# One PSUM row for the last group's weighted sums, and a pair tile for each pair sum, at the end of a summed-area-table diagonal kernel

## The chip, the cores and the metric

The kernel runs on one core of one Trainium2 chip. The metric is the device time of one execution in microseconds (us); the median of several executions is quoted. The span of a profile is shorter than that time, mostly by about 1.7 us, so spans are compared with spans and times with times.

## The reference

```python
B, H, W = 4, 4224, 4224          # x: float32, normally distributed
ps = np.cumsum(np.cumsum(x, axis=1), axis=2)
diag = np.diagonal(ps, axis1=1, axis2=2)
return np.cumsum(diag, axis=1).astype(np.float32)      # 4 x 4224
```

Element (i, j) of a matrix enters every diagonal place k with k >= max(i, j), and so enters place n of the output n + 1 - max(i, j) times. The work is to read 285 MB once and add it up by max(i, j).

## The kernel before: the parts that matter

A strip of 768 rows is loaded as bf16 (the load converts: the page of before counts 285.47 MB read from memory and 143.27 MB in the packets, about half). TensorE sums its columns right of the diagonal block, ScalarE and VectorE sum its rows left of it, and a masked product by VectorE splits the diagonal block. The outputs are worked out in 11 groups of 384 places.

The last group of the last matrix has a path of its own, since nothing can follow its loads but what still has to be done with them. Its first 256 rows are `part_a` (two loads). Its last 128 rows are `part_b`: four blocks of 32 rows (0 to 3), each row spread over four partitions as 1024 columns. Blocks 0 to 2 have one load each, block 3 has two (768 columns, then 256). A row's total is multiplied by a row of weights in a matmul with one output partition ("weighing"), the products gather in PSUM (where this kernel's matmuls put their results, `fin_a`, `fin_m` and `fin_e` below), and VectorE adds the gathered row to what the earlier rows gave (`c12`) and hands it to the store.

```python
def act_sum(acc, src):                        # ScalarE: sum along a row
    ...
def pair_sum(acc, src):                       # VectorE: sum along a row, two halves at a time
    w = src.shape[-1] // 2
    pair = dumpool.tile([P, 512], FP32, name="pair")     # ONE buffer for all pair sums
    nc.vector.scalar_tensor_tensor(out=pair[:, :w], in0=src[:, :w], scalar=1.0,
        in1=src[:, w:], op0=ALU.mult, op1=ALU.add, accum_out=acc)

# ... rows before the last 128: folded by TensorE 128 columns at a time
fold_a = psum_s.tile([P, 2, P], FP32, name="fold_a")
fold_in(fold_a, part_a, c0, cp, P, start=True)
# ... cut: the two scans and the output of the earlier groups ...

fin_a = psum_s.tile([1, M0], FP32, name="fin_a")         # places 0..255
fin_m = psum_s.tile([1, E0 - M0], FP32, name="fin_m")    # places 256..351
fin_e = psum_s.tile([1, R], FP32, name="fin_e")          # places 352..383
# ... cut: block 0 and half of block 1 folded by TensorE with weights, result `by` ...
fins = ((fin_a, 0, M0), (fin_m, M0, E0), (fin_e, E0, GW))
weigh(arows[:, 0:1], weights, 0, fins[:1], start=True)
# ... six more calls, each of one matmul per row that it touches ...
finish(fin_a, 0, M0)                                     # VectorE: 256-place addition
act_sum(bsum[:, 1:2], part_b[:, 2, :448])                # block 2
pair_sum(bsum[:, 2:3], part_b[:, 2, 448:])
for k in (1, 2):
    weigh(bsum[:, k : k + 1], weights4, M0 + 2 * R, fins)

act_sum(esum[:, 0:1], part_b[:, 3, :320])                # block 3
pair_sum(esum[:, 1:2], part_b[:, 3, 320:bcut])           # "first pair sum"
pair_sum(esum[:, 2:3], part_b[:, 3, bcut:])              # "second pair sum", the last load
for k in (1, 0, 2):
    weigh(esum[:, k : k + 1], weights4, E0, fins)
finish(fin_m, M0, E0)
# ... store of places 0..351 ...
finish(fin_e, E0, GW)
# ... store of places 352..383, the last instruction but for the end
```

## Time and profile before

| | before |
|---|---|
| time, median of 6 runs | 668.55 us (668.1 to 669.11); 668.58 of the first three |
| span of the profiled run | 666.7 us |
| DMA engines | full in every slice of the page but the last (9, then 8 tenths), 428 GB/s read |
| last load's landing, to the issue of the last store | 663.753 to 664.765: 1.012 us |
| issue of the last store, to the end of the kernel | 1.943 us |

The third row says that nothing but the load matters until the last load lands. The two rows under it are all that a change at the end can shorten. A landing is read from the record of the semaphore that the load raises. The measure "landing of the last load to the issue of the last store" leaves out when the stream happened to end.

### The profile page before, as it was taken

Reading aid. Unit: us, or ns where it says so; the run is one execution under the profiler, and the core shown is the slowest. Engines: PE = TensorE matmul, PEld = TensorE weight load, DVE = VectorE, ACT = ScalarE, POOL = GpSimd, SP = SyncE. Lnnn points to the kernel's source line nnn. Section 1 sums busy time; section 2 is a strip of 40 time slices with the busy share of each in tenths; the row PEclk is TensorE's granted clock in tenths of the full one; section 3 lists DMA queues with packets and bytes.
Section 4 is the critical chain, followed back from the end, with each engine's and each line's share of the span. In section 5 each row is a group of like instructions: output and inputs, shape, how many; then the busy total and the mean of one; then the engine's idle time right before and its main releaser. Section 6 shows DMA issues by size and latency. Waiting matters only on the chain.

```text
span 666.7 us, 2921 instructions
## 1 busy us (share of the span) xinstructions
PE 215.4 (32%) x1009; PEld 99.4 (15%) x1009; DVE 335.7 (50%) x381; ACT 140.2 (21%) x226; POOL 28.0 (4%) x61
## 2 busy tenths in 40 slices
PE   0071623403118153140321724404032254350426
PEld 0030211101003021010110312201011021120103
DVE  3023627276924351745782425265498241635776
ACT  0000121406300103040630020304063002030436
POOL 5000000000000000000000000000000000001000
PEclk9995858566558585765655958667565595765759
DMA  9999999999999999999999999999999999999998
GB/s 201 219 219 219 214 219 218 211 217 213 218 220 219 216 217 219 216 217 219 214 216 216 216 219 217 220 211 219 217 217 219 213 220 215 217 217 217 215 210 154
DMA packets 7673, 143.27 MB, mean 215 GB/s; under 512 B 702, under 2 KB 1002, under 8 KB 2154
## 3 DMA queue, kind: packets, MB, share of 16 engines
q0 software_dynamic: 7296, 142.47, 99.8%
q1 hardware_dynamic: 362, 0.61, 0.3%
q8 instruction: 8, 0.13, 0.1%
q14 instruction: 7, 0.06, 0.0%
HBM read 285.47 MB, written 0.07 MB: 428 GB/s over the span
## 4 chain that ended last, share of the span: by engine, by line
another core or an unknown queue 39%; DVE 24%; PE 21%; DMA 12%; issue 4%; POOL 0%; DVEq 0%; POOLq 0%
PE d L214 21%; DVE acc L240 16%; DMA strip<-in_x_dram 12%; DVE mu L257 6%; POOL strip L420 0%; DVE pu L240 0%; DVE c L257 0%; POOL strip L409 0%; DVE acc L343 0%; DVE acc L340 0%; PE carry_ps L214 0%; DVE rows L368 0%; DVEq L257 0%; PE fin_e L214 0%
## 5 line engine op out<-in xcount | busy, mean ns | idle before, releaser
L257 DVE SCALAR_TENSOR_TENSOR mu<-strip,um 128x768 bf16<-128x768 bf16 (+1 forms) x129 | 110.7, 908 | 308.9 <-DMA strip<-in_x_dram 217.6
L214 PE MATMUL d<-strip,sel 128*11 128x384 bf16 x603 | 138.9, 404 | 333.8 <-DMA strip<-in_x_dram 333.8
L235 ACT ACTIVATE dump<-strip 128x416 bf16<-128x416 bf16 (+8 forms) x112 | 128.3, 1146 | 523.0 <-DMA strip<-in_x_dram 520.3
L240 DVE TENSOR_REDUCE acc<-strip 128x6 f32<-128x4608 bf16 (+6 forms) x23 | 195.9, 8519 | 0.0
L214 PEld LDWEIGHTS <-sel 128*11 128x11 bf16 x849 | 86.2, 102 | 512.9 <-issue 475.3
L214 PE MATMUL d<-mu,sel 128*11 128x384 bf16 x243 | 59.6, 354 | 65.7 <-DVE mu L257 65.5
L76 POOL DMA_DIRECT2D strip<-in_x_dram x24 | 16.4, 686 | 555.9 <-DVE acc L240 415.4
L235 ACT ACTIVATION_READ_ACCUMULATOR dump<-strip 128x1 f32 x112 | 20.9, 186 | 0.0
L214 PE MATMUL d<-ident,rows 128*11 128x128 f32 x24 | 5.2, 379 | 17.2 <-DVE rows L377 16.4
L257 DVE DVE_READ_ACCUMULATOR mu<-strip,um 128x1 f32 x129 | 10.6, 82 | 0.0
L214 PE MATMUL fold<-strip,ident_h 128*128 128x480 bf16 x8 | 3.3, 589 | 8.6 <-DMA strip<-in_x_dram 8.6
L214 PEld LDWEIGHTS d<-ident,rows 128*11 128x11 f32 x24 | 2.5, 119 | 19.1 <-DVE rows L377 17.3
L214 PE MATMUL d<-halves,rows 128*11 128x64 f32 x48 | 5.3, 290 | 0.0
L214 PEld LDWEIGHTS d<-halves,rows 128*11 128x11 f32 x48 | 4.7, 127 | 1.8 <-issue 1.7
L240 DVE TENSOR_REDUCE pu<-d 11x1 f32<-11x384 f32 x4 | 2.2, 545 | 5.0 <-PE d L214 5.0
L214 PE MATMUL fold<-weights,quarter 32*128 32x128 f32 x2 | 0.8, 498 | 11.0 <-POOL quarter L200 11.0
L447 DVE TENSOR_TENSOR_SCAN c<-ones_row,carry,c 11x384 f32<-11x384 f32 x4 | 4.0, 1006 | 0.1
L447 DVE TENSOR_TENSOR_SCAN c<-ones_row,carry,d 11x384 f32<-11x384 f32 x4 | 4.0, 1001 | 0.1
L214 PEld LDWEIGHTS <-ident_h 128*128 128x128 bf16 x20 | 2.2, 114 | 12.0 <-issue 11.9
L420 POOL DMA_DIRECT2D strip<-in_x_dram x5 | 2.7, 552 | 21.5 <-DMA strip<-in_x_dram 21.5
L240 DVE TENSOR_REDUCE parts<-strip 128x3 f32<-128x3072 bf16 x1 | 3.4, 3350 | 0.0
L221 DVE COPY weights<-fold 128x128 f32<-128x128 f32 x1 | 0.3, 291 | 5.4 <-PE fold L214 5.4
(102 smaller groups left out, 44.4 us busy)
## 6 DMA issues: line engine op xcount, KB each, us to landing
strip<-in_x_dram POOLq DMA_DIRECT2D x19, 6336.0 KB, 69.2
strip<-in_x_dram POOLq DMA_DIRECT2D x5, 3168.0 KB, 55.2
strip<-in_x_dram POOLq DMA_DIRECT2D x1, 1080.0 KB, 45.0
strip<-in_x_dram POOLq DMA_DIRECT2D x1, 768.0 KB, 48.0
strip<-in_x_dram POOLq DMA_DIRECT2D x3, 256.0 KB, 49.2
head<-in_x_dram SPq DMA_DIRECT2D x1, 528.0 KB, 3.9
strip<-in_x_dram POOLq DMA_DIRECT2D x1, 192.0 KB, 43.7
strip<-in_x_dram POOLq DMA_DIRECT2D x1, 64.0 KB, 28.6
```

The costliest lines, as they stand in the source:

```text
L76: nc.gpsimd.dma_start(out=o, in_=x[b, r0 : r0 + f * P, :].rearrange("(p f) w -> p f w", f=f))
L214: nc.tensor.matmul(o, lhsT=lhsT, rhs=rhs, start=start, stop=False, skip_group_check=True)
L221: nc.vector.tensor_copy(out=weights4, in_=w4_ps)
L235: nc.scalar.activation(out=dump[:, :w], in_=src, func=ACT.Copy, accum_out=acc)
L240: nc.vector.reduce_sum(out=acc, in_=src, axis=AX.X)
L257: nc.vector.scalar_tensor_tensor(out=o, in0=i, scalar=1.0, in1=m, op0=ALU.mult, op1=ALU.mult, accum_out=acc,)
L420: nc.gpsimd.dma_start(out=part_b[:, sb, c0:c1], in_=x[b, r0 : r0 + R, :TB].rearrange("r (k c) -> r k c", k=4)[:, :, c0:c1],)
L447: nc.vector.tensor_tensor_scan(out=c12[:, i, :], data0=ones_row, data1=src, initial=carry[:, i : i + 1], op0=ALU.mult, op1=ALU.add,)
```

## The change

The intent is to have less in front of the last pair sums. All weighted sums but block 3's gather in one PSUM row, so that each total is weighed by one matmul instead of up to three. The rows of `part_a` are folded 256 columns at a time (folding: TensorE adds slices of so many columns onto one another in PSUM, which leaves one slice for VectorE to sum up). Block 1 is summed by ScalarE and VectorE instead of half by TensorE. The addition of the first 256 places moves behind block 2's pair sum. Each pair sum writes a tile of its own.

```diff
+    pairs = []
     def pair_sum(acc, src):
         w = src.shape[-1] // 2
-        pair = dumpool.tile([P, 512], FP32, name="pair")
+        pair = last.tile([P, 288], FP32, name=f"pair{len(pairs)}")
+        pairs.append(pair)
@@ part_a
-            fold_a = psum_s.tile([P, 2, P], FP32, name="fold_a")
+            fold_a = psum_s.tile([P, 2, 256], FP32, name="fold_a")
-            fold_in(fold_a, part_a, c0, cp, P, start=True)
+            fold_in(fold_a, part_a, c0, cp, 256, start=True)
   (and the same for the second load)
@@ last group
-        fin_a = psum_s.tile([1, M0], FP32, name="fin_a")
-        fin_m = psum_s.tile([1, E0 - M0], FP32, name="fin_m")
+        fin = psum_s.tile([1, GW], FP32, name="fin")
   (weigh: one matmul into fin[:, r0:]; finish(c0, c1) adds fin[:, c0:c1])
-        c1a = CB // 2
-        for sb, cp in ((0, CB), (1, c1a)):
-            ... four matmuls of block 1 among them ...
+        for c in range(0, CB, P):
+            matmul(by_ps, part_b[:, 0, c : c + P], weights4_h, start=c == 0)
   ...
-        finish(fin_a, 0, M0)
-        act_sum(bsum[:, 1:2], part_b[:, 2, :448])
-        pair_sum(bsum[:, 2:3], part_b[:, 2, 448:])
-        for k in (1, 2):
-            weigh(bsum[:, k : k + 1], weights4, M0 + 2 * R, fins)
+        for k, ca in ((0, 512), (1, 448)):
+            act_sum(bsum[:, k, 0:1], part_b[:, k + 1, :ca])
+            pair_sum(bsum[:, k, 1:2], part_b[:, k + 1, ca:])
+            if k == 1:
+                finish(0, M0)
+            row_sums(btot[:, k : k + 1], bsum[:, k])
+            weigh(btot[:, k : k + 1], weights4, M0 + (k + 1) * R)
   ...
-            weigh(esum[:, k : k + 1], weights4, E0, fins)
-        finish(fin_m, M0, E0)
+            matmul(fin_e, esum[:, k : k + 1], weights4[:, :R], start=k == 1)
+        finish(M0, GW)
   ...
-        finish(fin_e, E0, GW)
+        ye = last.tile([1, R], FP32, name="ye")
+        nc.vector.tensor_add(out=ye, in0=fin_e, in1=yl[:, E0:])
```

## The prediction

> **What bounds the kernel now.** I read the page first: slices, queues, memory traffic.
>
> ```profile
> DMA  9999999999999999999999999999999999999998
> q0 software_dynamic: 7296, 142.47, 99.8%
> q8 instruction: 8, 0.13, 0.1%
> HBM read 285.47 MB, written 0.07 MB: 428 GB/s over the span
> ```
>
> The reader is to see that the DMA engines are full in every slice: the load of x is 285.47 MB, and 285.47 MB at 428 GB/s is the whole span of 666.7 us. VectorE is busy 50%, TensorE 32%. So the change, which touches only the last group of the last matrix, cannot move the body. All that is left to it is the stretch between the landing of the last loads and the end. The table by windows shows how short that is (its columns are span, then busy time and count of TensorE, weight loads, VectorE, ScalarE, GpSimd, then granted clock, DMA share, GB/s).
>
> ```profile
> 662.00:663.00 1.00, 1.00 (x19) 0.95 (x18) 0.63 (x2) 0.59 (x3) 0.00 (x0) 1.00 0.58 93
> 663.00:664.00 1.00, 0.72 (x18) 0.55 (x15) 0.61 (x5) 0.74 (x4) 0.00 (x0) 1.00 0.04 6
> 664.00:665.00 1.00, 0.52 (x6) 0.22 (x6) 0.58 (x4) 0.06 (x1) 0.00 (x0) 1.00 0.00 0
> ```
>
> The stream stops a little after 663; what follows is tail. The chain of waits, from 663 us, says what the tail is made of (start, length, what):
>
> ```profile
> 619.74 43.68 DMA strip<-in_x_dram
> 663.51 0.29 DVE pair L246
> 663.83 0.10 DVE pair L246
> 663.97 0.57 PE fin_e L214 x6
> 664.56 0.18 DVE yl L491
> ```
>
> The fourth of the five block loads (block 3, first 768 places) lands at 663.42, then come VectorE's pair sums, TensorE's weighing, VectorE's addition and the store. The VectorE and SyncE timelines give the steps:
>
> ```profile
> 662.37 0.41 DVE L491 TENSOR_TENSOR yl<-fin_a,c 1x256 f32<-1x256 f32 x1 [1.48 <-PE fin_a L214]
> 662.71 0.44 DVE L246 SCALAR_TENSOR_TENSOR pair<-strip 128x288 f32<-128x288 bf16 x1
> 663.51 0.39 DVE L246 SCALAR_TENSOR_TENSOR pair<-strip 128x224 f32<-128x224 bf16 x1 [0.36 <-DMA strip<-in_x_dram]
> 663.83 0.08 DVE L246 DVE_READ_ACCUMULATOR pair<-strip 128x1 f32 x1
> 663.95 0.29 DVE L246 SCALAR_TENSOR_TENSOR pair<-strip 128x128 f32<-128x128 bf16 x1
> 664.16 0.08 DVE L246 DVE_READ_ACCUMULATOR pair<-strip 128x1 f32 x1
> 664.56 0.18 DVE L491 TENSOR_TENSOR yl<-fin_e,c 1x32 f32<-1x32 f32 x1 [0.15 <-PE fin_e L214]
> 664.76 0.23 SPq L540 DMA_DIRECT2D out_dram<-yl  x1
> ```
>
> Two things count here. First, the last load (64 KB) was issued at 635.17 and took 28.6 us in the list of DMA issues, so it landed at 663.75; the last pair sum starts only at 663.95. It waited not for data but for the pair sum before it, whose accumulator read ends at 663.91: both write the one tile "pair", and the order of instructions shows that wait. Second, I looked at the single packets behind the window's 0.58 DMA share. The eight fetches of queue 8 are 16,384 B each, and they start when TensorE has run 189, 456, 707, 948, 1216, 1467, 1705 and 1962 matmuls and weight loads: every 256 or so. So I take them for TensorE's own instructions (16,384/256 = 64 B each). The last one runs from 662.337 to 663.768, in the middle of the last loads. Fifteen of the sixteen engines have their final load packet done by 662.97; one goes on to 663.46, beside that fetch. From last packet to landing is 663.75 - 663.46 = 0.29 us, so without the slow engine the last load would have landed near 662.97 + 0.29 = 663.26, and the load before it near 662.59 + 0.30 = 662.89 instead of 663.42.
>
> [...]
> [...]
> [...]the engine with the fetch takes 0.041 us per 512 B packet at the end and the last fetch takes 1.43 us where the seven before took 0.89 to 0.97.
> [...]in the strips the next masked product starts with the accumulator read (639.69 and 639.69), while the pair sum with a wait starts 663.95 - 663.83 = 0.12 us after it.
> [...]
>
> **The change part by part.**
>
> *Folding 256 places at a time.* Twelve 256-column matmuls (0.27 us each, 0.11 apart) become six of 512 columns: the same column count, so about the same end, 659.57. VectorE's sum of fold_a grows from 256 to 512 elements: by the other PSUM sum (480 elements, 0.65 us) about 0.69 instead of 0.39. It starts at 660.15, so the row totals come at about 661.04 instead of 660.89. Before, TensorE started on them only at 661.52, since block 1's half fold came first; now that fold is gone. No loss.
>
> *One row "fin".* Sixteen weighing matmuls ahead of block 3 become six. An fp32 matmul runs in two passes; 256 columns start 0.215 us apart, 0.84 ns a column and pass. Now 384+256+128+128 columns cost 896 x 1.68 ns = 1.5 us, from 661.09 to about 662.6; the two block sums (96 and 64 columns) add 0.16 and 0.11. Before, TensorE was at it until 663.69. All this ends before it is needed.
>
> *Block 1 by both.* Four matmuls leave, a pair sum (about 0.40 us, 661.24 to 661.65) and a 2-element sum (0.16) come. ScalarE's half is unchanged: 512 elements, read by 662.00. VectorE was idle from 660.89 to 662.37. Free.
>
> *Block 2.* The 288-wide pair sum now comes ahead of the 256-place addition: from 662.53 (landing 662.49 plus 0.04) instead of 662.71, its accumulator read at 662.91; the addition takes its place in the pipe from 662.91 to 663.25 (next start 0.34 later, as 662.37 to 662.71); the block total needs ScalarE's sum (663.24) and starts near 663.28, next start at about 663.36. This is VectorE's new load ahead of block 3: it is 0.06 us short of the old landing.
>
> *Block 3.* Each pair sum has its own tile, so the 0.12 us wait goes, and with it a separate semaphore step. With the landings as before: first pair at 663.46, its read at 663.78; second at 663.80, read done at 664.10 instead of 664.25. TensorE's last weighing follows in 0.05 and takes 0.22 (664.30 to 664.52 now), but it must also pass ScalarE's part (read by 664.06): end about 664.40. VectorE's 128-place addition (by 96 at 0.24 and 256 at 0.41, about 0.275) runs from 664.02 and is hidden; the last addition runs 664.43 to 664.61, the store goes at 664.64 instead of 664.765. Gain 0.12 us.
>
> *The fetch.* TensorE's stream shrinks: 6 fold matmuls and 4 half-fold matmuls with their loads (20 instructions) and 10 weighing matmuls at 4 instructions (40), together 60. The fetch came at count 1962 of about 2018; the new stream ends near 1958. So at the same count the fetch falls at or behind the last matmul, after the loads. Then the loads land at about 662.89 and 663.26, and VectorE is the bound: first pair 663.36, second 663.68, read done 663.98, weighing done 664.26, last addition 664.29 to 664.47, store at 664.50. Gain 0.27 us.
>
> The store's end to the kernel's end stays as it is. Sum: 0.27 if the fetch leaves, 0.12 if it stays. I hold the first at 65%[...]: 0.65 x 0.27 + 0.35 x 0.12 = 0.22 us; 668.58 - 0.22 = 668.36, and the profiled run (668.42) hints that the median lies a shade high. I say 668.3.
>
> **The rivals.**
> 1. *Hidden anyway.* The chain is paced by the landing and the 0.12 us wait is not real: the time stays 668.6. For it: the stream fills every slice. Against: the 0.20 us between the last landing and the last pair sum.
> 2. *VectorE becomes the bound for the worse.* The addition of 256 places and the block totals stand in front of block 3, in order. If the 256-place addition waits for block 1's weighing, or the total of block 2 comes late by ScalarE, the first pair slips past 663.51 by 0.1 to 0.3 us: 668.7 to 668.9. Against: every input is due 0.06 us or more ahead.
> 3. *The fetch stays inside the loads,*[...]: 668.45[...].
>
> **Range and chances.** The three runs before spread 0.83 us (668.11 to 668.94), more than any of these effects. A median of three from that spread is good to some 0.25 us, two of them compared to 0.35, with the mechanisms 0.37; eight times in ten that is 0.47 either way. So 668.3, from 667.8 to 668.8. Two per cent are 13.4 us, ten times the whole tail: faster 0.01, same 0.985, slower 0.005.
>
> **What would show it.** Right: same DMA rate in the slices; no instruction packet of queue 8 between 662 and 663.5; last two landings near 662.9 and 663.3; the second block-3 pair sum starting with the accumulator read of the first, not 0.12 later; store issue near 664.5 relative to a block-2 landing at 662.49. Wrong: VectorE idle ahead of block 3's first pair with ScalarE named as releaser; a gap between the two pair sums; the fetch still there; or a body that has moved by more than half a microsecond, which this working has no cause for.

The sum: 0.27 us if the fetch leaves and 0.12 us if it stays, 0.65 x 0.27 + 0.35 x 0.12 = 0.22 us, and 668.58 - 0.22 = 668.36, given as 668.3.

## The result, and the profile after

| | before | after |
|---|---|---|
| time, median of 6 runs | 668.55 us (668.1 to 669.11) | 668.34 us (668.02 to 669.51) |
| span of the profiled run | 666.7 us | 666.4 us |
| block 2 lands | 662.490 | 662.304 |
| block 3's loads land behind that | 0.928 and 1.263 | 0.925 and 1.264 |
| last landing to last store | 1.012 | 0.881 |
| last store to the end | 1.943 | 1.952 |

The ratio of the times is 1.0001, with a 95% interval from 0.9988 to 1.0014: the same. A ratio here is the mean time of one kernel's fast runs over that of the other's fast runs of the same rounds, so it is not quite the ratio of the medians. The six runs after are 668.11, 668.02, 668.27, 669.48, 669.51 and 668.41, two of them over 1 us above the rest.

The 0.31 us between the two spans come apart by subtraction: the loads as a whole ended 0.185 us earlier (663.568 against 663.753), the tail is 0.131 us shorter, and the end 0.009 us longer. No load was changed and the whole run-to-run spread is larger than the first of these, so only the second is credited to the change.

The page of before, first its counts of instructions by engine, and then the same line and the queue of TensorE's instruction fetches after:

```profile
PE 215.4 (32%) x1009; PEld 99.4 (15%) x1009; DVE 335.7 (50%) x381; ACT 140.2 (21%) x226; POOL 28.0 (4%) x61
```

```profile
PE 213.0 (32%) x979; PEld 96.8 (15%) x979; DVE 336.7 (51%) x385; ACT 140.2 (21%) x226; POOL 28.0 (4%) x61
...
q8 instruction: 7, 0.11, 0.1%
```

TensorE has 30 matmuls and 30 weight loads fewer, 60 as predicted, and the eighth fetch is gone, as predicted. (An fp32 weighing is listed as two matmuls with a weight load each: before, the one on `dtot` into `fin_m` is `fin_m<-weights,dtot` x2, and its loads are x2.) The windows of the changed kernel; the first line belongs to a question taken up further below (the clock), the other three answer to the windows in the prediction:

```profile
658.06:661.47 3.41, 1.96 (x13) 0.81 (x13) 3.11 (x6) 2.46 (x6) 0.00 (x0) 1.00 1.12 205
...
662.00:663.00 1.00, 0.78 (x7) 0.42 (x5) 0.66 (x4) 0.61 (x2) 0.00 (x0) 1.00 0.36 53
663.00:664.00 1.00, 0.56 (x7) 0.25 (x8) 1.00 (x7) 0.62 (x3) 0.00 (x0) 1.00 0.03 5
664.00:665.00 1.00, 0.21 (x4) 0.07 (x4) 0.26 (x2) 0.00 (x0) 0.00 (x0) 1.00 0.00 1
```

TensorE was busy all of 662 to 663 with 19 matmuls before, and has 7 there now. VectorE, in turn, is at 1.00 from 663 to 664: it has become the engine of that stretch. The timeline of the changed kernel (start, length, engine, line, operation, tiles, and in brackets what ended an idle time before it) shows in which order:

```profile
660.93 1.24 PE L214 MATMUL fin<-weights,arows 128*1 128x384 f32 x4 [0.51 <-DVE arows L240]
...
662.33 0.46 DVE L249 SCALAR_TENSOR_TENSOR pair<-strip 128x288 f32<-128x288 bf16 x1 [0.32 <-DMA strip<-in_x_dram]
...
662.81 0.41 DVE L488 TENSOR_TENSOR yl<-fin,c 1x256 f32<-1x256 f32 x1
663.15 0.13 DVE L240 TENSOR_REDUCE btot<-bsum 128x1 f32<-128x2 f32 x1
663.25 0.39 DVE L249 SCALAR_TENSOR_TENSOR pair<-strip 128x224 f32<-128x224 bf16 x1
663.57 0.08 DVE L249 DVE_READ_ACCUMULATOR pair<-strip 128x1 f32 x1
663.59 0.29 DVE L249 SCALAR_TENSOR_TENSOR pair<-strip 128x128 f32<-128x128 bf16 x1
...
664.24 0.18 DVE L527 TENSOR_TENSOR ye<-fin_e,yl 1x32 f32<-1x32 f32 x1 [0.16 <-PE fin_e L214]
```

An accumulator read is the short instruction behind a pair sum that writes the sum out (0.07 to 0.08 us here). The second pair sum (663.59) starts 0.02 us after the first one's accumulator read (663.57); before it started 0.12 us after it. Block 3's first load lands at 663.229, 0.024 us before the first pair sum, and block 2's total (`btot`, 663.15) sits directly in front. So nothing is to spare there. The chain of waits, followed back from the end, agrees:

```profile
663.15 0.13 DVE btot L240
663.29 0.38 DVE pair L249 x2
...
663.71 0.22 PE fin_e L214 x2
...
663.93 0.29 PE fin_e L214 x4
...
664.24 0.18 DVE ye L527
```

TensorE weighs block 3's totals in two steps: the last four matmuls wait for ScalarE's part of block 3 and for the second pair sum, which come at nearly the same moment (ScalarE's read ends at 663.875). So the tail has two branches of about the same length now, and the 0.12 us wait of the prediction is not won in full on either of them alone.

### The profile page after: what moved, and what is told of

It is laid out like the page before. It is cut to its first block, busy times and chain, and to the rows that moved or that the text cites. A ratio compares the mean times of both kernels' runs of the same rounds, so it can differ in the third digit from the quotient of the medians.

```text
span 666.4 us, 2866 instructions
## 1 busy us (share of the span) xinstructions
PE 213.0 (32%) x979; PEld 96.8 (15%) x979; DVE 336.7 (51%) x385; ACT 140.2 (21%) x226; POOL 28.0 (4%) x61
## 4 chain that ended last, share of the span: by engine, by line
another core or an unknown queue 38%; DVE 24%; PE 21%; DMA 13%; issue 4%; POOL 0%; ACT 0%; DVEq 0%; POOLq 0%; ACTq 0%
PE d L214 21%; DVE acc L240 16%; DMA strip<-in_x_dram 13%; DVE mu L260 6%; DVE pu L240 0%; DVE c L260 0%; POOL strip L412 0%; DVE acc L346 0%; DVE acc L343 0%; DVE pair L249 0%; ACT dump L235 0%; PE carry_ps L214 0%; DVE rows L371 0%; DVEq L260 0%
```

## The experiments

Twelve runs were made. Those of one batch (e1 to e4, r5 to r8, r9 to r12) shared one chip each. All but r5, r6, r7 and r12 are single runs, so their state is unknown; where a verdict rests on their traces, distances to a landing are used and not times.

The theory after the first look: the tail gain of 0.13 us comes from the pair tiles and from VectorE no longer stepping through a separate semaphore wait (`DVEq L246`, 0.02 us at 663.45 in the chain of before; the chain of after has none); the rest of the change (row, folding, block 1, moved addition) adds nothing to the end; and the fetch was never what held the late loads. Rivals: the row or the reordering made the gain; or the fetch did matter, and something else took its place.

### e1: the changed kernel with one shared pair tile again

```diff
-        pair = last.tile([P, 288], FP32, name=f"pair{len(pairs)}")
-        pairs.append(pair)
+        pair = dumpool.tile([P, 512], FP32, name="pair")
```

> Measure: from the landing of the last load (block 3, last 256 places) to the issue of the last store; before 1.01 us, after 0.88 us. Here the changed kernel with one shared tile for all pair sums again. Theory (the gain is the write-after-write wait on that tile): the second block-3 pair sum starts 0.03 us behind the first's accumulator read, not during it, so 0.10 us later; TensorE's last weighing, which after the change also waits on ScalarE's part, ends 0.05 to 0.10 later: 0.93 to 0.98 us. Rival (one row, fewer matmuls, reordering make the gain): stays at 0.88. The whole time, 668.3 to 668.6, cannot tell them apart.

Measured: 668.11 us (the kernel before, on the same chip: 668.83, one run each). Last landing to last store: 0.937 us, against 0.881 with own tiles. Its VectorE timeline:

```profile
663.17 0.39 DVE L248 SCALAR_TENSOR_TENSOR pair<-strip 128x224 f32<-128x224 bf16 x1
663.49 0.08 DVE L248 DVE_READ_ACCUMULATOR pair<-strip 128x1 f32 x1
663.60 0.29 DVE L248 SCALAR_TENSOR_TENSOR pair<-strip 128x128 f32<-128x128 bf16 x1
```

The wait between the pair sums is back: 663.60 - 663.49 is 0.11 (0.119 in the records), though block 3's second load had landed at 663.485. So the wait comes from the shared tile, not from the data. It costs 0.10 us at the second pair sum's end and 0.056 us at the store, since ScalarE's branch takes up the difference. The first pair sum still starts 0.024 us behind its landing, where the kernel before needed 0.093: that other 0.07 us does not need the separate tiles. A likely reason, not shown by a run: in the new order the instruction in front is block 2's total, which comes behind the earlier pair sum and its accumulator read anyway. So the 0.131 us are 0.056 from the tiles and 0.075 from the rest, most of it this earlier start.

### e2: the kernel before with own pair tiles

```diff
+    pairs = []
-        pair = dumpool.tile([P, 512], FP32, name="pair")
+        pair = last.tile([P, 288], FP32, name=f"pair{len(pairs)}")
+        pairs.append(pair)
```

> The kernel before with nothing changed but a tile of its own for each of its three pair sums. Theory: the wait goes, the second block-3 pair sum starts within 0.03 to 0.08 us of the landing (before 0.19), and landing to last store falls from 1.01 to 0.87 to 0.92 us, the whole gain of the change. Rival (the row and the fewer matmuls make it): stays within 0.03 of 1.01. The fetch of TensorE instructions stays in the tail, near 662.3 us.

Measured: 668.69 us. Last landing to last store: 0.844 us, so even a little less than the changed kernel's 0.881. The first pair sum starts 0.024 us behind its landing, so own tiles take away that 0.07 us too: either the tiles or the new order is enough for it. The timeline of this run also shows why it can't count in full:

```profile
663.64 0.39 DVE L249 SCALAR_TENSOR_TENSOR pair<-strip 128x224 f32<-128x224 bf16 x1 [0.24 <-DMA strip<-in_x_dram]
...
664.21 0.29 DVE L249 SCALAR_TENSOR_TENSOR pair<-strip 128x128 f32<-128x128 bf16 x1 [0.17 <-DMA strip<-in_x_dram]
```

The last load landed late here, 1.511 us behind block 2 instead of 1.263, and both pair sums waited for data. The first one's read was over at 664.04, before the second landing at 664.188, so a shared tile would not have held the second one either. What the run does show: the old rows, folding and order, left as they were, allow a tail as short as the changed kernel's when the last load lands this late. With the usual 1.26 us TensorE would have had 0.25 us less for its weighing; that case was not run.

The packets of this trace tell where those 0.25 us come from, for the most part. The eighth fetch of TensorE's instructions, expected near 662.3 us, started at 663.671, 0.003 us behind the last load packet of the last engine, and the landing followed that packet's start by 0.520 us. In the other thirteen traces no fetch stands there, and it follows by 0.315 to 0.347. So a fetch directly behind the last packet probably held this landing by about 0.2 us. It is one trace, and no run placed a fetch there on purpose.

### e3: the changed kernel with 32 small matmuls early

This puts TensorE's instruction count back up, so that the eighth fetch returns among the last loads. The early matmuls lie where TensorE is idle.

```diff
+    early = psum_s.tile([NG, NG], FP32, name="early")
+    for i in range(32):
+        matmul(early, sel[:, :NG], sel[:, :NG], start=i == 0)
     ones_col = consts.tile([P, 1], FP32, name="ones_col")
```

> The changed kernel with 32 small matmuls (64 TensorE instructions) of no use while TensorE waits for the first load, so that the eighth fetch of its instructions is due again in the tail, near 662.0 to 662.5 us. My prediction said that this fetch made the last DMA engine late; then the last two landings come later again, by 0.3 to 0.5 us against the landing of block 2 (after: 0.93 and 1.26 us behind it). Rival, from the trace after the change, where the fetch is gone and the engine as late as before: the lag is older than the tail, and the last two land 0.93 and 1.26 us behind block 2, within 0.05. Landing to last store 0.88 in both.

Measured: 670.66 us. The fetch is back (eight of them, the last from 661.50). Block 3's loads land 0.930 and 1.266 us behind block 2's. Without the fetch it was 0.925 and 1.264. But the fetch ended at 662.446, 1.18 us ahead of block 2's landing (663.622), so it missed the place that it was meant for. Two later runs came nearer: r9 had it at 662.19, 0.41 us ahead of block 2's landing, with 0.922 and 1.268; r10 at 662.06, 0.18 us ahead (0.15 in the kernel before), with 0.928 and 1.263. So a fetch beside the late packets does not make these loads late, and its absence does not bring them forward: the prediction's largest term is refuted from both sides. Only e2's fetch, directly behind the last packet, goes with a later landing.

Not expected was the time. Last landing to last store took 2.110 us instead of 0.88, and the window table gives a granted TensorE clock of 0.50 for 662 to 664. The next run has the same.

### e4: the changed kernel with a second 256-place addition

The aim was VectorE's slack in front of block 3: one more instruction of 0.34 us there, where the sum of the prediction has 0.06 us to spare.

```diff
             if k == 1:
                 finish(0, M0)
+                spare = last.tile([1, M0], FP32, name="spare")
+                nc.vector.tensor_add(out=spare, in0=fin[:, :M0], in1=c12[0:1, 1, :M0])
```

> The changed kernel with the 256-place addition done twice on VectorE, ahead of block 2's total (0.34 us more). Theory: VectorE has no room left ahead of block 3 (its first pair sum began 0.02 us after landing, right behind block 2's total), so that pair sum slips by 0.30 to 0.34 us and landing to last store grows from 0.88 to 1.03 to 1.22 us. Rival (VectorE has slack and the loads set the end): within 0.05 of 0.88.

Measured: 669.89 us, last landing to last store 2.732 us. One window that ends where the clock fell (660.77), and two after it:

```profile
657.36:660.77 3.41, 1.66 (x15) 0.90 (x15) 2.88 (x5) 2.09 (x5) 0.00 (x0) 1.00 1.12 209
...
661.00:662.00 1.00, 1.00 (x2) 0.13 (x1) 0.52 (x3) 0.72 (x2) 0.00 (x0) 0.50 0.89 150
662.00:663.00 1.00, 1.00 (x4) 0.31 (x3) 0.47 (x2) 0.67 (x2) 0.00 (x0) 0.50 0.26 38
```

The timeline of TensorE and VectorE in this run:

```profile
660.85 2.29 PE L214 MATMUL fin<-weights,arows 128*1 128x384 f32 x4 [0.53 <-DVE arows L240]
...
664.36 0.41 DVE L488 TENSOR_TENSOR yl<-fin,c 1x256 f32<-1x256 f32 x1 [1.67 <-PE fin L214]
```

The four weighing matmuls took 2.29 us instead of 1.24, and VectorE stood idle 1.67 us in front of the 256-place addition, with TensorE named as releaser. Block 3 lay landed all that time, behind the addition. So this run says nothing of VectorE's slack (that was tried again as r11), but shows a second thing that decides the tail: the granted clock.

The traces have two granted clocks, 0.50 and 1.00, and no other. The changes lie on a grid: in the kernel before the clock changes at 622.20, 629.03, 652.92 and 666.58 us, distances of 2, 7 and 4 steps of 3.41 us. Such a step is called a window here. Where the grid lies differs between executions, of one kernel too (a window ends at 661.47 us in the changed kernel and at 661.95 in r5, the same kernel), so the window that decides about the tail falls differently in each one.

| run, unfilled | window ending ahead of the tail | TensorE busy in it | clock after |
|---|---|---|---|
| e4 | 657.36 to 660.77 | 1.66 us | 0.50 |
| r8 | 658.11 to 661.52 | 1.67 | 0.50 |
| e3 | 658.21 to 661.62 | 1.73 | 0.50 |
| r5 (below) | 658.54 to 661.95 | 1.77 | 1.00 |
| after | 658.06 to 661.47 | 1.96 | 1.00 |
| e1 | 656.08 to 659.49 | 1.96 | 1.00 |
| before | 656.34 to 659.75 | 1.99 | 1.00 |
| e2 | 659.02 to 662.43 | 2.31 | 1.00 |

How busy is busy enough? In these windows the line lies near half: behind one with 1.73 us of 3.41 the clock fell and behind one with 1.77 it did not. It is not a sharp one. Counted over all 722 windows at full clock in the fourteen traces, those with more than 1.89 us of matmuls kept the clock and those with less than 1.60 lost it; of the 31 between, 28 lost it and 3 kept it (one of them with 1.61, in r12; one with 1.89 lost it, in the kernel before). Of 1844 windows at half clock, none with less than 2.62 us was followed by full clock and all with more than 2.72 were. The ends of matmuls are modelled and some records can be missing. At the phases of e3, e4 and r8, relative to block 2's landing, the kernel before would have had 1.55 to 1.75 us in its window and the changed kernel 1.66 to 1.73 (read from their own traces). So by this count both are exposed alike. Of the six unfilled traces of the changed kernel and its variants three have the half clock (e3, e4, r8); of the two unfilled ones of the kernel before none has.

### r5: the changed kernel again, five rounds

No edit.

> The changed kernel unaltered, five more rounds. In the traces with 32 extra matmuls and with the second addition the granted clock fell to 0.50 for one 3.41 us stretch inside the tail, and the weighing took twice as long. Theory: the changed kernel's six times fall in two groups for that reason (668.0 to 668.4 four times, 669.5 twice), so here again about a third of the runs is 1.2 to 1.5 us above the others. Rival (the two high times were chance in the loads): a single spread of some 0.8 us without a gap.

Measured, on another chip: 668.78, 670.99, 668.97, 668.36, 669.06 and 670.50 us; the kernel before 668.31 to 669.96, median 669.17 of 11. Ratio 1.0007 (0.9994 to 1.002). Again two of six are more than 1.4 us above the others. Over both sets that is four of twelve. The profiled run of this set had clock 1.00 in the tail and a distance from last landing to last store of 0.884 us, so the 0.88 repeats. That the high runs are the half-clock ones fits by size (e3's tail is 1.23 us longer than the changed kernel's, r8's 1.45), but timed runs leave no trace, so it isn't shown. Their mean clock over the whole span doesn't separate them: 0.658 to 0.663 in the four high runs, 0.659 to 0.665 in the other eight.

### r6 and r7: filled kernels

Nine matmuls without a use are put into the idle times of TensorE before the tail, in the changed kernel (r6) and in the kernel before (r7). They were meant to lie in front of nothing that is waited for (r11 has a reservation).

```diff
+    def keep_busy(o, n):
+        for i in range(n):
+            matmul(o, sel[:, :NG], um6[0][:, :GW], start=True)
   (for the last matrix: 2 behind the first fold of part_a, 4 behind the
    carry matmuls, 1 behind the second fold, 2 behind block 0's fold)
```

> The changed kernel with nine idle-time matmuls of no use (384 columns, 0.16 us each) in four waits of TensorE between 656.9 and 660.9 us, so that no 3.41 us stretch there is mostly idle. Theory (a stretch with little TensorE work halves the clock of the next, and that makes the high times): granted clock 1.00 in the whole tail, all five times within 667.8 to 668.6, landing to last store 0.88 us as before. Rival (chance in the loads): a third of the times stays at 669.5; or the fillings get in the way and landing to last store grows by over 0.05.

> The kernel before with the same nine matmuls in the same waits. Theory: its high times (669.11 of six) go as well, all five between 668.0 and 668.8, and its mean lies 0.05 to 0.3 us above that of the changed kernel with the fillings, the 0.13 us of the tail; landing to last store 1.01 us. Rival (the change wins or loses more than its tail shows): the means of the two filled kernels are more than 0.4 us apart.

Measured: r6 669.05, 668.40, 669.63, 669.01 and 669.46 us, ratio 1.0000 (0.9988 to 1.0012); r7 668.98, 669.11, 669.74, 668.34 and 668.78 us, ratio 0.9998 (0.9986 to 1.001). Both traces have clock 1.00 in the tail. The window of r6 that decides about the tail ends 2.3 us ahead of block 2's landing, nearly where e3's did (2.0):

```profile
657.52:660.93 3.41, 3.13 (x20) 1.08 (x19) 2.92 (x7) 2.23 (x5) 0.00 (x0) 1.00 1.12 208
```

TensorE is busy 3.13 us of 3.41 there, against e3's 1.73. So the filling does what it should to the clock. The tails are 0.845 us (r6) and 0.968 us (r7): a difference of 0.123, which repeats the 0.131 in another pair of kernels. But both kernels' times miss what was expected of them (within 667.8 to 668.6, and 668.0 to 668.8): the whole chip was slower than the first, and the runs spread by 1.2 and 1.4 us without a gap. No filled run of the ten is a clear outlier, against four of twelve unfilled ones of the changed kernel; with numbers so small that is a hint and no more. The filled kernels' means, 669.11 and 668.99, come out in the wrong order for the tail, by less than one run's spread; their mean spans, 667.14 and 667.24, come out in the right order, with no more weight.

### r8: 130 small VectorE instructions early

If the fetch isn't what makes one DMA engine late, what is? The trace doesn't number the engines, but it has the final packet of each engine in each load, and how far one lies behind the first of the sixteen. These distances are carried on from load to load unchanged (in the kernel before the last engine is 1.72 us behind the first in each of the six loads from 365 to 499 us), so an engine can be followed by its distance. In the load that ends at 655 us the last engine is 2.12 us behind the first in the kernel before. One engine's distance grows in steps of about 0.53 us, each time that 8,192 B of instructions are fetched for VectorE (fetches start at VectorE's counts of 70, 195, 321 and 450, waits and other sequencer instructions counted). With 130 more VectorE instructions, one more such fetch has to fall into the loads.

```diff
+    tiny = consts.tile([P, 130], FP32, name="tiny")
+    for i in range(130):
+        nc.vector.memset(tiny[:, i : i + 1], 0.0)
     ones_col = consts.tile([P, 1], FP32, name="ones_col")
```

> The changed kernel with 130 one-column fills on VectorE while it waits for the first load. In all six traces the fetches of 8,192 B that come each 128 VectorE instructions put one and the same DMA engine back by 0.53 us each; four of them make it the last one, about 2.0 us behind the first. Theory: a fifth fetch makes the gap between the first and the last engine's final packets of one load, measured behind 630 us, 2.5 to 2.6 us instead of 1.96 to 2.13, and the last load lands 0.5 us later. Rival (fetches of instructions do not matter, as the failed step of my prediction would have it in general): the gap stays at 1.9 to 2.2.

Measured, from the final packets of each load, how far the engine that ends up last was behind the first of the sixteen:

```
load landing near     34     125    290    485    635 us
e1 (four fetches)    0.00   0.53   1.00   1.53   2.07
r8 (five fetches)    0.64   1.16   1.69   2.22   2.75
```

The extra fetch came at 17 us, in the first load, and the engine was 0.64 us behind from there on, with the same four steps on top: 2.75 us before the last loads: above the 2.5 to 2.6 of the theory, since the first distance was 0.64, and clear of the rival's 2.2. So instruction fetches of VectorE hold one and the same engine, 0.53 us each. In nine of the fourteen traces that engine is the last one at 655 us. In the other five (e2, r6, r7, r11, r12) another is, and fetches of other engines set back DMA engines too: in e1 no engine is over 0.45 us behind in the load that lands at 64 us, and one is 1.30 us behind in that of 95 us, with TensorE's first fetch (from 69.5 to 70.5 us) between them and none of VectorE's. TensorE's seven or eight fetches don't add up on one engine as VectorE's do: seven steps of e1's size, 0.85 us or more, would make 6 us, and in the kernel before, with seven of them by 655 us, no engine is over 2.12 us behind the first. The start is different in each run: the last engine was 0.45 to 2.63 us behind at the first load. Over the fourteen traces the last engine's distance in the load near 655 us (1.96 to 3.35 us) and the landing of the last load (663.46 to 664.89) go together with a correlation of 0.90 and 0.95 us of landing per us of distance. That is what a late engine, and not a late packet, would give. It is a correlation over different kernels and several chips, and r8 alone raised one of the two on purpose. Its last load landed at 664.007, 0.44 us later than in the changed kernel, where 0.5 was expected; but r5, with no edit, has 664.231, so the one run doesn't show that part. The time, 670.03 us, is no measure of that: this run had the half clock (0.50 from 661.52), and a tail of 2.327 us.

### r9 and r10: every weighing issued twice

To try the mechanism of e3 and e4 without waiting for a slow clock: on the filled kernels, whose clock is 1.00, each weighing matmul is issued a second time into a spare PSUM tile. That about doubles the weighing, as the half clock did (2.29 us against 1.24 for the first four matmuls in e4).

```diff
             matmul(fin[:, r0:], rows, w[:, : GW - r0], start=start)
+            matmul(busy[0:1, r0:], rows, w[:, : GW - r0], start=True)
   (and the same behind block 3's three; in r10 behind each matmul of weigh)
```

> The filled changed kernel (clock held at 1.00) with every weighing matmul of the last group issued a second time onto an unused row, so that the weighing takes twice as long, as at half the clock. Theory: in the changed kernel the 256-place addition waits for the whole row and stands on VectorE ahead of block 3, so slow weighing stops the pair sums: landing to last store grows from 0.85-0.88 to 2.0 to 2.5 us, the first block-3 pair sum starts 1.1 to 1.6 us behind its landing, and VectorE names the row as what it waited for. Rival (the high times have another cause than slow weighing): below 1.4 us.

> The same doubling in the filled kernel before. Theory: three separate rows let the first 256 places be finished early, so block 3's pair sums stay within 0.2 us of their landings, but TensorE itself is late: its 1,120 columns take 3.8 us from 661.5 and the last weighing ends near 1.9 us behind the last landing: landing to last store 1.9 to 2.3 us. So both kernels lose over 1 us in that state, the changed one 0.1 to 0.4 more. Rival (only the changed kernel loses): before stays under 1.3 us.

Measured: r9 669.81 us with a tail of 2.285 us; r10 669.55 us with a tail of 2.357 us (1.9 to 2.3 was expected). VectorE's timeline in r9:

```profile
664.62 0.41 DVE L498 TENSOR_TENSOR yl<-fin,c 1x256 f32<-1x256 f32 x1 [1.53 <-PE fin L214]
```

and in r10:

```profile
663.80 0.29 DVE L246 SCALAR_TENSOR_TENSOR pair<-strip 128x128 f32<-128x128 bf16 x1
...
665.18 0.25 DVE L503 TENSOR_TENSOR yl<-fin_m,c 1x96 f32<-1x96 f32 x1 [1.08 <-PE fin_m L214]
```

In the changed kernel VectorE waits for the row in front of the 256-place addition, and block 3's pair sums stand behind it: they start 1.50 us after their landing. That is e4's picture at full clock, so slow weighing alone makes it. In the kernel before the pair sums run in time (0.30 us after the landing), but TensorE itself is late with all its weighing, 2.11 us behind the landing. The excess over the filled kernels is 1.44 us (2.285 - 0.845) after and 1.39 us (2.357 - 0.968) before: the same but for 0.05. I had expected the kernel before to lose 0.1 to 0.4 us less. So the moved addition makes VectorE wait, but the changed kernel as a whole loses no more by slow weighing than the kernel before. What it would lose with the addition in its old place was not run.

### r11: the second addition on the filled kernel

The edit of e4, on r6.

> The filled changed kernel with the 256-place addition done twice, as the earlier run of that kind fell into the half clock and told nothing of VectorE. Theory: with the clock at 1.00 the first block-3 pair sum slips by 0.28 to 0.34 us and landing to last store grows from 0.85-0.88 to 1.03 to 1.22 us. Rival (VectorE had slack): within 0.05 of 0.88.

Measured: 668.96 us; last landing to last store 1.417 us, above both what the theory (1.03 to 1.22) and the rival (0.93 at most) had. VectorE:

```profile
663.45 0.41 DVE L497 TENSOR_TENSOR yl<-fin,c 1x256 f32<-1x256 f32 x1 [0.41 <-PE fin L214]
663.79 0.40 DVE L523 TENSOR_TENSOR spare<-fin,c 1x256 f32<-1x256 f32 x1
```

The second addition takes 0.34 us (663.79 to 664.13, the start of the next). The rest of the 0.57 us over r6's 0.845 belongs to the 0.41 us that VectorE waited for the row: `part_a`'s totals came late in this run, because VectorE was still at the scans until 660.6 (1.9 us ahead of block 2's landing, against 2.3 in r6). The first pair sum starts 0.70 us behind its landing instead of 0.02. So there is no slack in front of block 3, against the rival, and the row comes only just in time in general. How much of it is which can't be told more closely than this from one run.

### r12: a version meant to beat both

The filled changed kernel with fewer VectorE instructions (more buffers for the masked products with small marker copies, meant to save most of the 121 wait instructions among VectorE's 509 in the trace of the changed kernel), so that the fourth VectorE fetch falls behind the end.

```diff
-    mup = ctx.enter_context(tc.tile_pool(name="mup", bufs=3))
+    mup = ctx.enter_context(tc.tile_pool(name="mup", bufs=6))
+    mark = consts.tile([P, 1], FP32, name="mark")
   (in add_up, behind row_sums)
+            if f == F2:
+                nc.vector.tensor_copy(out=mark, in_=acc[:, f - 1, 1:2])
```

> A version meant to beat both: the filled changed kernel with six instead of three buffers for the masked products and one 1-element copy on VectorE behind each six-row strip's sum, by which some 100 separate waits on VectorE's own results drop out of its instruction stream and some 20 copies come in: about 430 instructions instead of 509. Theory: the fourth fetch of VectorE's instructions, at count 450, does not come; the engine it would put back by 0.53 us is the last one in most traces, so the gap between first and last engine behind 630 us falls from about 2.0 to 1.4-1.6 us (more where the first load alone set one engine back), and the mean time falls by 0.3 to 0.7 us against the filled kernel and by 0.5 to 1.0 us against before. Rival (another engine is as late, or VectorE's added copies cost): gap and mean within 0.25 us of the filled kernel's.

Measured: 668.84, 669.86, 669.81, 670.55, 668.36 and 669.53 us, median 669.67; the kernel before on the same chip 668.13 to 670.68, median 668.98 of 11. Ratio 1.001 (0.9996 to 1.0023). The fourth fetch did go, and the step of 0.53 us between 619 and 635 us with it. But in the traced run another engine was 2.58 us behind at the first load and still 2.16 at 655 us (1.4 to 1.6 was expected), so the loads ended no earlier. The tail is 0.899 us. The version doesn't beat either kernel. It also has runs over 1 us above its lowest, though filled, so the clock may not be the only source of those; no trace shows these runs. And the kernel before has one as well: 670.68 of the 11, 1.7 us above their median.

## Why the prediction was right or wrong

The time was predicted as 668.3 and came as 668.34, inside the range, and the class was right for the reason given: the full DMA engines, which a change in the tail can't touch. That the medians fell by 0.21 us where 0.22 was forecast is luck: the means of the same runs differ by 0.07 us the other way, and two of the terms below were wrong. Step by step:

- **Folding, row, block 1.** Right. The fold sum took 0.66 us (predicted 0.69), block 1's pair sum 0.43 (0.40), its total 0.15 (0.16), and all of it ended before it was needed. By e2 none of it was needed for a short tail, at least with a last landing as late as there.
- **Block 2.** Right, but tighter than written. Block 2's total was to leave 0.06 us; it left nothing, as the first pair sum starts 0.024 us behind the landing and in r11 a second addition of 0.34 us there, with a late row, put the first pair sum 0.70 us behind its landing. The rival "VectorE becomes the bound" was nearer than its words: what it feared, the 256-place addition waiting for the row, happened where weighing was slow (1.38 us in e3, 1.67 in e4, 1.53 in r9).
- **Block 3.** Right in sum: store 0.89 us behind the landing if the landings stay (664.64 - 663.75), measured 0.881. That is 0.131 us gained where 0.12 was predicted. Wrong in its sources: the tile's wait is real (e1: 0.119 against 0.021), but brings only 0.056 at the store, and the other 0.075 is mostly the 0.07 us step of the first pair sum, which own tiles take away (e2) but the new order takes away as well (e1).
- **The fetch.** This is the step that failed. The count was right: 60 instructions fewer, and the eighth fetch gone. But "without the slow engine the last load would have landed near 662.97 + 0.29 = 663.26, and the load before it near" 662.89 took a fetch that lay beside the late packets for the reason of their lateness. The loads landed 0.925 and 1.264 us behind block 2 after it was gone, 0.922 to 0.928 and 1.263 to 1.268 with it back in that place (r9, r10). The packet time that was set beside the fetch, 0.041 us per 512 B on the last engine, is that of engines with no fetch as well (661.301, 661.343, then the final packet at 661.384, in the same trace). The long last fetch, 1.43 us, was not explained. These distances are just what the bytes need: block 3's first load reads 768 x 128 x 4 B = 0.393 MB, which at 428 GB/s is 0.92 us, and the second 0.131 MB, 0.31 us (0.339 measured). So an engine that is late is late in every block load by the same amount (here the last one ends block 3's two loads at 663.089 and 663.438, each 0.49 us behind the engine before it, as at 655 us), and works without a pause in between; the prediction's 662.89 would have been 0.40 us behind block 2's landing, too little for those bytes at that rate, unless block 2 had landed earlier too. In the fetch's place: engines start out at different distances in each run, and one of them, the last one in this trace, falls behind by 0.53 us with each VectorE fetch (r8). The term "Gain 0.27 us" was therefore 0.12, and the expected value of 0.22 us should have been 0.12: 668.46, within the same range. A fetch can still hold a landing when it comes directly behind the last packet (e2, about 0.2 us), which is not what the prediction described. What could have been seen beforehand in the trace of before: the last engine was 2.12 us behind the first in the load at 655 us already, seven microseconds ahead of that fetch.
- **What was left out.** The clock. The prediction's table has a granted clock of 1.00 for the tail, and I took that as given. Half the unfilled traces of the changed kernel and its variants have 0.50 there, at 1.2 to 1.9 us longer tails (all three are of variants, none of the two of the kernel itself). That is about ten times the gain, and would be reason enough why a gain of 0.13 us doesn't show in the means (ratio 1.0001).
- **Rivals.** "Hidden anyway" is refuted for the tail (0.131, and 0.123 in the filled pair, one trace each; the changed kernel's was repeated in r5), though in the time of whole runs it can't be told from what happened. "The fetch stays" is refuted: it left.

What stays open: whether the four high runs of twelve are the half-clock ones; a half-clock tail of the kernel before, which by r10 and the window count should exist, was in no trace; why the engines are apart at the first load, which engine a TensorE fetch falls on, by how much a late engine sets the end (r12 took one step of 0.53 us away, but drew a bad first load); and whether the filling, or fewer VectorE instructions, is worth anything in the mean. All kernels that were timed in rounds lie within about 0.1% of each other, which is as fine as these runs can tell.

## What to carry to other kernels

Give scratch outputs that nobody reads their own tiles when the instructions that write them stand in the tail: here a shared one made VectorE wait for itself, 0.10 us (0.119 against 0.021 behind the accumulator read). Before one late transfer is put down to what lies beside it, look at whether the same DMA engine was already late in the loads before (here 2.12 us at 655 us). An effect of a tenth of a microsecond in a run that varies by a whole one is to be read from the trace as a distance to the event that starts it (here the last landing), and the granted clock of that stretch is to be compared first.
